# Releasing a pair's attention behind the next block's keys and values in a fused decoder block

## The chip, the core and the metric

The kernel runs on one core of one Trainium2 chip. The metric is the device time of one execution in microseconds (us), lower is better. Engines are named as the profile names them: PE (TensorE, matmuls and transposes; PEld its weight loads), DVE (VectorE), ACT (ScalarE), POOL (GpSimd), SP (SyncE, which issues most DMAs). The program gives each engine its instructions in a fixed order.

## The reference

One decoder layer on 2048 tokens of width 1024, in float32:

```python
h = modulate(rms_norm(x, g_pre_mix), shift_m, scale_m)
proj = h @ w_in          # q_a k_a v_a | q_m k_m v_m o_m | i_m f_m | g_a g_m
q_a, k_a = rope(q_a), rope(k_a)                     # 8 query heads, 2 key heads, 64 wide
y_a = sliding_window_attention(q_a, k_a, v_a, sinks)  # window 128, blocks of 128 tokens
q_m, k_m = silu(causal_conv4(q_m, k_m))
h_m = mlstm_chunkwise(q_m, k_m, v_m, i_m + b_i, f_m + b_f)   # 4 heads, 128 wide
y_m = sigmoid(o_m) * head_layer_norm(h_m)
merged = sigmoid(g_a) * (y_a @ w_branch_attn) + sigmoid(g_m) * (y_m @ w_branch_mlstm)
x = x + gate_m * rms_norm(merged @ w_out)
h2 = modulate(rms_norm(x, g_pre_ffn), shift_f, scale_f)
x = x + gate_f * rms_norm((silu(h2 @ w_ffn_gate) * (h2 @ w_ffn_up)) @ w_ffn_down)
```

A query block of 128 tokens attends to its own keys and those of the block before. The mLSTM's input and forget gates i and f go through a log-sigmoid, a cumulative sum and a running maximum over the tokens before its chunks can start.

## The kernel before

**Precision.** Each float32 operand is split into a high part (a cast on ACT, lines 264, 267 and 1744) and a low part (a subtraction on DVE, lines 265, 268 and 1745); a product is three matmuls (`mm3`), recorded at line 212. Transposes are recorded at line 217.

**Staging.** The tokens are four blocks of 512 (b = 0 to 3), taken in two superblocks sb of a pair b0, b1. `superblock(sb)` is a list of work items in program order: queries of b0 (q0), keys, values and gate pre-activations of b0 (kv0, 264 columns), the mLSTM values of b0 (`vm(b0)`), then kv1, q1 and `vm(b1)` for the other block, then 14 pairs of projection columns (`pairs`, each with a two-by-two fast product over both blocks), then both blocks' outputs. In the first superblock q0 and kv0 were written by hand in `first_block`. A group such as kv1 is `KD * NT` = 32 products of three matmuls, 96 matmuls in all.

**Weights.** In the first two blocks weights come from the inputs, are split and the parts of b1 are stored to HBM (line 374, `w_kv_d`, `w_q_d`, `w_vm_d`); in superblock 1 they are loaded ready split (lines 328 and 333). All these go out on SP's queue in its order. There are two raw buffers (`raw`) and four buffers for split parts (`whi`, `wlo`).

**Attention.** When a token tile of q or k/v leaves its accumulator, a stream rotates it on DVE (`rope`, lines 790 to 793), transposes it on PE and stores it into a per-block tile in HBM, `at_d[n]` (lines 806, 833, 851 and 853). `attend(b)` first forces all these streams to their end (`finish(R["qk"])`), then makes the four 128-token attention blocks of b ready; for b0 it also spawns two `attention_stream`s, one for the even and one for the odd blocks, so that attention runs in pairs of 128-token blocks. A block loads its tile (`at`, line 954, 896 KB, two buffers; line 949 and 952 for the very first), computes 24 score matmuls (`mix<-at`), copies and masks them (lines 985 and 987), takes maxima (993), exponentials on ACT (1002), sums (1003, 1004), a scaling on POOL (1005), transposes, masks (1014, 1018), does the value matmuls (`mix<-tm,at`) and stores `y_d` (1032, 1037). If the block two places on is already released, its tile is loaded at once, from ACT's queue; otherwise the stream waits and loads it from SP's.

**Gates.** `attend(b)` also spawns `gates(b)`: small DVE and ACT operations on `gt`, four transposes, the scans (lines 905 and 909 to 912), transposes of 68 rows and a few exponentials. It reads `gt`, which the next block's k/v evictions overwrite, so it has to come before them.

**What sets the order.** The program is written with a planner's clock: every matmul adds a planned time to `now`, and a spawned stream resumes once `now` has passed its due time (`tick`, the constants `L_...`), so its instructions are woven between the main matmuls. `finish` moves the clock forward until the given streams have ended. The tile framework then orders each engine's instructions by readiness on a modelled timeline, where of several that are ready the one earlier in the program goes first (`schedule_with_timeline_sim=True`); only the first block is held to program order. It also sets all waits.

**Where the results are needed.** `finish(convs + R["gs", b0] + R["gs", b1])` after the eighth projection pair, before the mLSTM starts; `end_attention(NT)` in the fourteenth pair, before `y_d` of b0 is loaded (line 1248); `end_attention(2 * NT)` later still.

**Buffers.** Attention, gates and the second conditioning stream (`ada_stream`, lines 467 and 476) share nine `tm` tiles; four PSUM banks serve as accumulators (`acc`) and four for everything else (`mix`).

Of the kernel before, what the change touches and what calls it, by code (L numbers as in the profile page):

```python
# [73 lines left out]
def decoder_block(ctx: ExitStack, tc: tile.TileContext, a: dict, out: bass.AP, dbg=None):  # L74
# [49 lines left out]
    def tx(shape, dtype=F32):  # L124
        return tpool.tile(shape, dtype, tag="tx", name=nm("tx"), bufs=9)
# [93 lines left out]
    def spawn(gen, delay=0.0):  # L219
        st = [now[0] + delay, gen, False]  # L220
        streams.append(st)
        return st
# [15 lines left out]
    def finish(sts):  # L238
        for st in sts:
            while not st[2]:  # L240
                now[0] = max(now[0], min(q[0] for q in streams))
                tick()
# [190 lines left out]
    b1 = const.tile([P, 48], F32, name="b1")  # L433
# [130 lines left out]
    def hsums(names):  # L564

        for name in names:
            raw = HR.pop(name)
            lo = hc_part(name, 1)
            nc.sync.dma_start(lo.bitcast(F32), raw)
        yield L_HD  # L570
        for name in names:
            hi, lo = (hc_part(name, i) for i in range(2))
            for k in range(4):
                v = lo[:, k, :].bitcast(F32)
                A.copy(hi[:, k, :], v)
                V.tensor_tensor(lo[:, k, :], v, hi[:, k, :].bitcast(F32), op=ALU.subtract)
                yield L_HS
# [191 lines left out]
    def superblock(sb):  # L769
        b0, b1 = 2 * sb, 2 * sb + 1  # L770
# [8 lines left out]
        def rope(raw, heads, b, t):  # L779
            sin, cos = tables[sb]  # L780
            t += (b % 2) * NT
            W = heads * HD
            raw = raw[:, :W]
            src = raw.rearrange("p (h u f) -> p h u f", u=2, f=32)
            cb = cos[:, t, :].unsqueeze(1).to_broadcast([P, heads * 2, 32])
            sb_ = sin[:, t, :].unsqueeze(1).unsqueeze(1).to_broadcast([P, heads, 2, 32])
            z = tx([P, 512])
            zz = z[:, :W].rearrange("p (h u f) -> p h u f", u=2, f=32)
            rr = raw.rearrange("p (h f) -> p h f", f=32)
            V.tensor_tensor(zz, src[:, :, ::-1, :], sb_, op=ALU.mult)  # L790
            V.tensor_tensor(rr, rr, cb, op=ALU.mult)
            V.tensor_tensor(src[:, :, 0, :], src[:, :, 0, :], zz[:, :, 0, :], op=ALU.subtract)
            V.tensor_tensor(src[:, :, 1, :], src[:, :, 1, :], zz[:, :, 1, :], op=ALU.add)
            return raw, z

        def q_stream(b, t, yz):
            yield L_ROPE
            y, z = yz
            pt = mix_tile()
            for j in range(GQ):  # L800
                transpose(pt[:, j * P:(j + 1) * P], y[:, j * P:(j + 1) * P])
            hi, lo = z.bitcast(F32R), y.bitcast(F32R)
            A.activation(hi, pt, AF.Copy, scale=HD ** -0.5)
            V.scalar_tensor_tensor(lo, pt, HD ** -0.5, hi.bitcast(F32), op0=ALU.mult, op1=ALU.subtract)
            for i, q in enumerate((hi, lo)):
                nc.sync.dma_start(at_d[b * NT + t][:, i * 512:(i + 1) * 512], q.bitcast(F32))
# [50 lines left out]
        def q_kv(b):  # L857
            if b > 1:
                q = token_group(kept_weights("q"), KD, 512, lhs_h(b), evac_q(b), kept=True)
            else:  # L860
                q = token_group(srcs_rows(w_in, KD, C_Q), KD, 512, lhs_h(b), evac_q(b), pair_heads=True, store="q" if b else None)
            if b > 1:
                return q, token_group(kept_weights("kv"), KD, 264, lhs_h(b), evac_kv(b), kept=True)
            raw_kv = Raw(load_kv)
            return q, token_group([(raw_kv, (lambda r, j=j: r[:, j:j + 2, :]), j, 2) for j in range(0, KD, 2)], KD, 264, lhs_h(b), evac_kv(b), store="kv" if b else None)

        def vm(b):
            def evac(t, ps):
                v = tx([P, 512])
                A.copy(v, ps)  # L870
                nc.sync.dma_start(vm_d[b][:, t, :], v)
            if b > 1:
                yield from token_group(kept_weights("vm"), KD, 512, lhs_h(b), evac, kept=True)
            else:
                yield from token_group(srcs_rows(w_in, KD, C_VM), KD, 512, lhs_h(b), evac, store="vm" if b else None)
# [69 lines left out]
        def load_at(n, queue):  # L945
            a_ = at()
            af = a_.bitcast(F32)
            if n == 0:
                queue.dma_start(af[:, :AT_K], at_d[n][:, :AT_K])
                for c0, k in ((AT_K, 2), (AT_V, 1)):  # L950
                    v_, d_ = (z[:, c0:c0 + 2 * k * P].rearrange("p (i u k) -> p i u k", i=k, u=2)[:, :, 1, :] for z in (af, at_d[n]))
                    queue.dma_start(v_, d_)
            else:
                queue.dma_start(af, at_d[n])
            return a_
# [86 lines left out]
        def attention_stream(u):  # L1042
            a_ = None
            for i in range(u, 2 * NT, 2):
                n = b0 * NT + i
                if a_ is None:
                    while i >= ready[0]:
                        yield 1000.0
                    a_ = load_at(n, nc.sync)
                    yield L_LOAD  # L1050
                    a_ = yield from attention(n, a_, lambda: i + 2 < ready[0])
                else:
                    yield L_LOAD - 1500.0
                    a_ = yield from attention(n, a_, lambda: i + 2 < ready[0])
                done_att[0] += 1
                yield 500.0
# [3 lines left out]
        def attend(b):  # L1060
            finish(R["qk"])
            ready[0] = (b - b0 + 1) * NT
            if b == b0:
                R["att"] = [spawn(attention_stream(0), L_QK), spawn(attention_stream(1), L_QK + L_ATT2)]
            R["gs", b] = [spawn(gates(b), L_QK)]

        def end_attention(n):
# [285 lines left out]
        if sb == 0:  # L1353
            raws, rotated = {}, {}

            def late_q(t):
                yield from q_stream(b0, t, rope(raws[t], HQ, b0, t))

            def q_raw(t, ps):
                raws[t] = tx([P, 512])  # L1360
                A.copy(raws[t], ps)
                if t > 1:
                    R["qk"].append(spawn(late_q(t), L_KV0 + L_LATE * (t - 1)))

            def q_rope(t):
                rotated[t] = rope(raws[t], HQ, b0, t)

            def q_rest(t):
                for _ in q_stream(b0, t, rotated[t]):
                    pass  # L1370

            first.update(kv=kv0, evac=q_raw, rope=q_rope, rest=q_rest)
        else:
            yield start
            yield from q0
            yield from kv0
            yield lambda: attend(b0)
        yield from vm(b0)
        yield lambda: finish([hps[b1]])
        if sb == 0:  # L1380
            yield lambda: attend(b0)
        yield lambda: hps.update(t=spawn(hsums(("T2", "T4"))))
        q1, kv1 = (list(z) for z in q_kv(b1))
        yield from kv1
        yield from q1
        vm1 = list(vm(b1))
        yield from vm1[:len(vm1) // 4]
        yield lambda: attend(b1)
        yield from vm1[len(vm1) // 4:]

        def start_f():
# [809 lines left out]
    def program():  # L2201
        items = [it for sb in range(NSB) for it in superblock(sb)]
        last = max(i for i, it in enumerate(items) if isinstance(it, Part))
        first_block()
        yield from items[:last]
        yield lambda: next(phase2)
        yield from items[last:]
# [47 lines left out]
```

## Time and profile before

| | us |
|---|---|
| median of 3 runs | 2666.65 |
| lowest, highest | 2666.62, 2668.6 |
| profiled execution, its own time | 2664.19 |
| profiled execution, span from first to last instruction | 2662.2 |
| PE busy in the span | 2614.5 (98%) |
| DVE busy in the span | 1935.3 (73%) |
| ACT busy in the span | 1281.4 (48%) |
| mean granted PE clock | 0.996 |

Times in the profile run from the first instruction of the span. A matmul row counts its modelled duration, and matmuls overlap, so the time from one to the next is read from runs of many in the chain of waits. "x24" counts instructions; `acc<-whi,big` reads "into an accumulator from a weight part and an activation part". A wait row names the engine, what it was to write and its line, then what it waited for.

By their rows the stages of interest lie so in the span: superblock 0 has `vm(b0)` from 74, kv1 from 97 to 119, q1 from 122; superblock 1 has kv0 to 735, `vm(b0)` to 763, kv1 from 766 to 784, q1 from 791 to 838.

### The profile page before, as it was taken

The page shows a single profiled execution, that of the slowest core. Times are in us where ns is not written, and L with a number is a line of the kernel's source. Part 1 is how long each engine was busy: PE and PEld are TensorE (multiplying, and loading weights), DVE is VectorE, ACT ScalarE, POOL GpSimd, SP SyncE. Part 2 cuts the span into 40 slices and gives each one's busy share as a digit, 9 for nine tenths or more (in the row PEclk, how much of TensorE's full clock was granted, in tenths as well). Part 3 has the DMA queues.
Part 4 walks back from the last instruction along what each step waited for, and adds up shares of the span by engine and source line. Part 5 has one row for each costly group of instructions (what it writes and reads, how often), then busy time and mean ns, then how long its engine had stood idle before and what let it go on. Part 6 is the DMA issues. An engine that isn't in the chain of part 4 may idle for free.

```text
span 2662.2 us, 36035 instructions
## 1 busy us (share of the span) xinstructions
PE 2614.5 (98%) x12546; PEld 2142.4 (80%) x12546; DVE 1935.3 (73%) x3758; ACT 1281.4 (48%) x2531; POOL 133.1 (5%) x181
## 2 busy tenths in 40 slices
PE   8999999999989999999999999999999999999998
PEld 6777788888877788888878888888778888888786
DVE  6878887768675988875877777776776767676466
ACT  6656544545654654454643433345544333333444
POOL 0000001101100000110000000000000000000000
PEclk9999999999999999999999999999999999999999
DMA  7794466897797545597766554547675323234556
GB/s 270 255 327 141 135 194 186 266 327 247 263 311 241 179 135 185 181 301 261 224 235 199 172 174 155 165 136 232 211 241 173 111 99 113 94 111 138 191 204 221
DMA packets 352166, 532.95 MB, mean 200 GB/s; under 512 B 23136, under 2 KB 209628, under 8 KB 345200
## 3 DMA queue, kind: packets, MB, share of 16 engines
q1 hardware_dynamic: 333768, 514.86, 57.8%
q10 hardware_dynamic: 18216, 15.79, 1.9%
q8 instruction: 99, 1.62, 0.2%
q14 instruction: 83, 0.68, 0.1%
HBM read 367.61 MB, written 154.57 MB: 196 GB/s over the span
## 4 chain that ended last, share of the span: by engine, by line
PE 88%; DVE 5%; DMA 4%; ACT 2%; issue 1%; POOL 0%; ACTq 0%; SPq 0%; DVEq 0%; POOLq 0%
PE acc L212 61%; PE mix L212 23%; PE mix L217 2%; DVE hl L1745 1%; PE acc L90 1%; PE mix L90 1%; ACT hl L1744 1%; DMA raw<-as_d 1%; ACT tm L1002 1%; DMA raw<-ws_d 0%; DMA raw<-w_kv_d 0%; DMA big<-in_x_dram 0%; DMA raw<-in_w_ffn_down_dram 0%; DMA at_d<-tx 0%; DMA raw<-in_w_in_dram 0%
## 5 line engine op out<-in xcount | busy, mean ns | idle before, releaser
L212 PE MATMUL acc<-big,hl 128*128 128x512 f32 x3936 | 936.0, 392 | 4.0 <-ACT hl L1744 1.8
L212 PEld LDWEIGHTS acc<-big,hl 128*128 128x128 f32 x3936 | 732.3, 188 | 164.4 <-issue 5.1
L1744 ACT CAST hl<-raw 128x512 fp32r<-128x512 f32 x732 | 439.9, 621 | 491.7 <-PE acc L212 216.3
L1745 DVE TENSOR_TENSOR hl<-raw,hl 128x512 fp32r<-128x512 f32 x732 | 496.6, 695 | 200.7 <-ACT hl L1744 197.1
L212 PE MATMUL acc<-whi,big 128*128 128x512 f32 (+1 forms) x896 | 279.3, 387 | 0.1
L212 PE MATMUL mix<-big,hl 128*128 128x512 f32 x1056 | 263.0, 390 | 1.8 <-ACT hl L1744 1.1
L212 PE MATMUL acc<-hl,hl 128*128 128x512 f32 x1008 | 237.3, 393 | 5.8 <-DVE hl L1745 3.0
L212 PEld LDWEIGHTS mix<-big,hl 128*128 128x128 f32 x1056 | 197.7, 188 | 44.6 <-ACT hl L1744 2.0
L212 PEld LDWEIGHTS acc<-hl,hl 128*128 128x128 f32 x1008 | 187.0, 188 | 51.5 <-DVE hl L1745 8.7
L212 PEld LDWEIGHTS acc<-whi,big 128*128 128x128 f32 x896 | 167.2, 189 | 33.3 <-ACT whi L264 0.4
L212 PE MATMUL mix<-hl,hl 128*128 128x512 f32 x792 | 182.6, 391 | 2.6 <-ACT hl L1744 1.8
L212 PEld LDWEIGHTS mix<-hl,hl 128*128 128x128 f32 x792 | 147.9, 188 | 36.5 <-ACT hl L1744 3.0
L212 PE MATMUL acc<-wlo,big 128*128 128x512 f32 (+1 forms) x448 | 173.4, 388 | 1.1 <-DVE wlo L265 1.1
L212 PE MATMUL acc<-big,whi 128*128 128x512 f32 x512 | 157.4, 393 | 0.0
L268 DVE TENSOR_TENSOR wlo<-raw,whi 128x1024 fp32r<-128x1024 f32 (+1 forms) x76 | 91.2, 1200 | 60.9 <-ACT whi L267 55.7
L267 ACT CAST whi<-raw 128x1024 fp32r<-128x1024 f32 (+1 forms) x76 | 78.3, 1031 | 93.9 <-PE acc L212 87.3
L492 POOL TENSOR_TENSOR rs<-ms,halves 128x1 f32<-128x1 f32 (+1 forms) x56 | 41.0, 739 | 1635.8 <-DVE ms L490 1589.2
L212 PE MATMUL mix<-hcT4h,hl 128*128 128x512 f32 x352 | 115.6, 389 | 0.7 <-ACT hl L1744 0.7
L212 PE MATMUL acc<-hcT2h,hl 128*128 128x512 f32 x352 | 115.5, 389 | 0.0
L212 PEld LDWEIGHTS acc<-big,whi 128*128 128x128 f32 x512 | 95.3, 188 | 19.3
L212 PEld LDWEIGHTS acc<-wlo,big 128*128 128x128 f32 x448 | 85.0, 190 | 18.8 <-DVE wlo L265 1.4
L212 PE MATMUL acc<-big,wlo 128*128 128x512 f32 x256 | 97.5, 392 | 0.0
(379 smaller groups left out, 3640.7 us busy)
## 6 DMA issues: line engine op xcount, KB each, us to landing
as_d<-w SPq DMA_DIRECT2D x154, 256.0 KB, 2.0
raw<-in_w_in_dram SPq DMA_DIRECT2D x36, 1024.0 KB, 5.4
raw<-as_d SPq DMA_DIRECT2D x70, 512.0 KB, 3.8
raw<-in_w_ffn_gate_dram SPq DMA_DIRECT2D x22, 1024.0 KB, 5.6
raw<-in_w_ffn_up_dram SPq DMA_DIRECT2D x22, 1024.0 KB, 6.0
raw<-ws_d SPq DMA_DIRECT2D x40, 512.0 KB, 4.7
tx<-in_w_ada_dram SPq DMA_DIRECT2D x64, 256.0 KB, 5.3
g_d<-tx SPq DMA_DIRECT2D x64, 256.0 KB, 4.5
```

The lines of the kernel that those rows point to most:

```text
L90: self.last = tc.keep_in_program_order(f(*p, **k)).ins
L212: T.matmul(o, lhsT=lhsT, rhs=rhs, start=start, stop=stop, skip_group_check=resumed)
L217: T.transpose(o, i, ident[:k, :k])
L267: A.copy(hv, src)
L268: V.tensor_tensor(lv, src, hv.bitcast(F32), op=ALU.subtract)
L492: G.tensor_tensor(r[:, :n], ms[:, :n], nhalf[:, :n], op=ALU.pow)
L1002: A.activation(sc[jj][:, i, :], sc[jj][:, i, :], AF.Exp, bias=nm_[:, c:c + 1], accum_out=sums[:, c:c + 1])
L1744: A.copy(v(hi), src)
L1745: V.tensor_tensor(v(lo), src, v(hi).bitcast(F32), op=ALU.subtract)
```

## The change

`attend(b)` is cut in two: `attend` keeps the forced finishing, the release and the two streams; the new `gate(b)` holds the spawning of `gates(b)`. Where `attend(b0)` stood, `gate(b0)` stands now: behind kv0 in superblock 1, behind `vm(b0)` in superblock 0. `attend(b0)` itself stands behind kv1 in both, ahead of q1. For b1 both are called where `attend(b1)` was, after the first quarter of `vm(b1)`.

```diff
             if b == b0:
                 R["att"] = [spawn(attention_stream(0), L_QK), spawn(attention_stream(1), L_QK + L_ATT2)]
+
+        def gate(b):
             R["gs", b] = [spawn(gates(b), L_QK)]
...
             yield from q0
             yield from kv0
-            yield lambda: attend(b0)
+            yield lambda: gate(b0)
         yield from vm(b0)
         yield lambda: finish([hps[b1]])
         if sb == 0:
-            yield lambda: attend(b0)
+            yield lambda: gate(b0)
         yield lambda: hps.update(t=spawn(hsums(("T2", "T4"))))
         q1, kv1 = (list(z) for z in q_kv(b1))
         yield from kv1
+        yield lambda: attend(b0)
         yield from q1
         vm1 = list(vm(b1))
         yield from vm1[:len(vm1) // 4]
-        yield lambda: attend(b1)
+        yield lambda: (attend(b1), gate(b1))
         yield from vm1[len(vm1) // 4:]
```

So the release of b0's attention moves past kv1 in superblock 0, and past `vm(b0)` and kv1 in superblock 1. The forced finishing at that place now also takes in the key streams of b1, which kv1 has just spawned. No instruction is added or removed.

## The prediction

> **What bounds the kernel now.** I read the page first, for what the end hangs on. Its first and fourth parts:
>
> ```profile
> PE 2614.5 (98%) x12546; PEld 2142.4 (80%) x12546; DVE 1935.3 (73%) x3758; ACT 1281.4 (48%) x2531; POOL 133.1 (5%) x181
> PE 88%; DVE 5%; DMA 4%; ACT 2%; issue 1%; POOL 0%; ACTq 0%; SPq 0%; DVEq 0%; POOLq 0%
> ```
>
> TensorE (PE) is the bound: 88% of the chain of waits is PE's own work. The change adds and removes no instruction of it, so it can win or lose only where PE stands still or runs at half clock. The second view is therefore the table of stretches around the moved work. Columns: length, then PE, PE weight loads, DVE, ACT and POOL busy, granted PE clock, DMA share, GB/s.
>
> ```profile
> 103.30:119.10 15.80, 14.17 (x104) 12.86 (x102) 13.10 (x40) 5.95 (x17) 0.00 (x0) 0.78 0.99 342
> 106.80:113.50 6.70, 5.77 (x32) 5.44 (x33) 6.58 (x19) 1.75 (x4) 0.00 (x0) 0.50 0.97 329
> 119.10:123.90 4.80, 1.35 (x8) 0.65 (x6) 2.91 (x12) 4.80 (x23) 2.19 (x2) 0.99 0.31 110
> 123.80:127.10 3.30, 3.24 (x10) 2.75 (x11) 2.19 (x10) 3.30 (x18) 1.56 (x2) 0.50 0.71 289
> 762.00:784.30 22.30, 19.25 (x131) 18.00 (x130) 16.29 (x51) 12.61 (x41) 2.35 (x2) 0.85 0.96 371
> 765.50:772.30 6.80, 6.13 (x35) 6.03 (x35) 4.79 (x10) 2.18 (x4) 0.00 (x0) 0.50 1.00 420
> 784.30:791.20 6.90, 3.91 (x30) 2.17 (x30) 6.44 (x31) 5.95 (x27) 1.14 (x2) 1.00 1.06 356
> 791.20:840.00 48.80, 48.80 (x276) 36.22 (x275) 23.48 (x62) 19.77 (x62) 5.63 (x6) 1.00 0.61 193
> 855.00:900.00 45.00, 42.99 (x230) 32.98 (x230) 44.19 (x98) 32.25 (x85) 4.28 (x4) 1.00 0.65 219
> ```
>
> PE idles 3.45 us in 119.1 to 123.9 (4.80 less 1.35), 2.99 us in 784.3 to 791.2, and three times its clock is 0.50. All this lies where the first pair of attention blocks of a superblock meets the other block's keys and values (kv1 below: 96 matmuls of 264 columns). Whom PE waited for, in the stretches 100 to 130, 755 to 792, 131 to 755 and 792 to 960, one fence each (total us, times, longest):
>
> ```profile
> PE mix L217 <- POOL tm L1005: 2.2, 1, 2.2
> PE mix L217 <- DVE tm L912: 1.6, 1, 1.6
> PE acc L212 <- DVE wlo L265: 1.1, 1, 1.1
> ```
>
> ```profile
> PE acc L212 <- DMA raw<-w_kv_d: 3.0, 1, 3.0
> PE mix L217 <- POOL tm L1005: 1.9, 1, 1.9
> PE mix L212 <- DVE tm L1018: 0.9, 2, 0.5
> PE mix L212 <- DMA at<-at_d: 0.9, 1, 0.9
> ```
>
> ```profile
> PE mix L217 <- POOL tm L1005: 1.7, 2, 1.3
> ```
>
> ```profile
> PE mix L217 <- POOL tm L1005: 0.3, 1, 0.3
> ```
>
> The softmax tail (L1005) holds PE 2.2 and 1.9 us at the two first pairs of a superblock, but 1.7 + 0.3 us at the six other pairs together with nothing else of attention: 0.33 us a pair. So a pair is cheap when it does not run beside kv1.
>
> What half clock costs is read from the chain of waits, where a piece is a run of matmuls of one kind:
>
> ```profile
> 108.42 2.86 PE mix L212 x18
> 111.28 4.13 PE acc L212 x24
> 123.86 1.65 PE acc L212 x3
> 126.57 2.65 PE acc L212 x10
> 143.22 3.50 PE mix L212 x33
> 286.39 67.79 PE acc L212 x298
> 766.17 4.30 PE acc L212 x18
> 770.92 2.26 PE mix L212 x18
> 778.48 6.06 PE acc L212 x48
> ```
>
> At full clock a matmul of 264 columns takes 0.126 us (6.06/48), one of 512 columns 0.227 (67.79/298), a score matmul 0.106 (3.50/33). So the half clock after 106.8 cost 4.13 - 24 x 0.126 = 1.1 and 2.86 - 18 x 0.106 = 0.95, that after 123.8 cost 1.65 - 3 x 0.227 = 0.97 and 2.65 - 10 x 0.227 = 0.4, together 3.4 us; that after 765.5 cost 2.0 + 0.35 = 2.4 us.
>
> **The change part by part.** *First superblock: scores move from inside kv1 to behind it.* kv1 is cut up by 48 score matmuls (24 a block). They bring DVE work, and the last weight split of kv1 stands behind it; the load of q1's first weights stands on SP behind the store of that split. DVE's groups in 108 to 114, and SP in time:
>
> ```profile
> L993 DVE TENSOR_REDUCE mx<-tm 128x4 f32<-128x512 f32 x3 | 2.0, 667 | 0.0
> L987 DVE COPY_PREDICATED_SCALAR tm<-m_prev,negc 128x256 f32 x4 | 1.7, 482 | 0.0
> L987 DVE COPY_PREDICATED tm<-m_prev,mix 128x256 f32<-128x256 uint32 x3 | 1.3, 425 | 0.0
> ```
>
> ```profile
> 114.57 0.32 SPq L374 DMA_DIRECT2D w_kv_d<-wlo  x1
> 114.94 0.43 SPq L298 DMA_DIRECT2D raw<-in_w_in_dram  x1
> ```
>
> Without those 5.0 us on DVE the split, the store and q1's weights come up to 5.0 us sooner, and the scores fill PE between kv1 and q1 instead of delaying both. Term 1, the idle 3.45: ends -3.45 and 0; I take -2.5, since DVE holds other work that moves up. Term 2, the half clocks, 3.4: ends -3.4 and 0; half, -1.7, as one of the two follows the wait for L1005 and L265, and the other the gates' wait. Term 3, that gates' wait (L912, 1.6): the gates keep their place, so 0; end -1.6.
>
> *Second superblock: past the values and kv1.* The two loads of attention tiles stand on SP just ahead of kv1's weights:
>
> ```profile
> 753.27 1.15 SPq L954 DMA_DIRECT2D at<-at_d  x2
> 754.48 0.43 SPq L333 DMA_DIRECT2D raw<-w_kv_d  x1
> ```
>
> ```profile
> at<-at_d SPq DMA_DIRECT2D x7, 896.0 KB, 8.1
> ```
>
> At the 371 GB/s of the table 896 KB last 2.5 us, so two loads hold the weights up by 4.9 us, more than the 3.0 us that PE waits for them. Term 4, the waits for these weights (3.0) and for the attention tile itself (0.9): at best both go, -3.9. If the weights land when they do now, the 0.9 becomes waiting for weights and the 24 scores that PE does ahead of them (2.5 us at 0.106) no longer fill that time: +2.5. I take -2.4, nearer to the first, since the loads then belong to later work. Term 5, the half clock after it, 2.4: ends -2.4 and 0; half, -1.2. Term 6, the idle 2.99 at 784.3, where kv1's evictions and rotations meet the softmax on DVE (6.44 of 6.90 busy): ends -2.99 and 0; -2.5, leaving what a pair costs elsewhere.
>
> *What the new place costs (term 7).* Two pairs run in q1, the second quarter of the values and the first projection pairs. At least 0.33 us each: +0.7; at most what their tails cost now, 3.45 + 2.99: +6.4. In 791 to 840 DVE has half its time free (23.48 of 48.80 busy), so I take +2.0, nearer the lower end.
>
> *At nothing.* The forced finishing now takes kv1's key streams behind kv1: four transposes, eight small ACT and DVE operations and eight stores. q1's matmuls, ready by then, hide them; without that cover PE waits for the four key rotations, which are less than the 6.44 us of DVE work in 784.3 to 791.2 that holds them: say +4. In the second superblock block b0's q and k streams are no longer forced ahead of the values; the 96 matmuls there cover them as now. The gates' DVE chain loses its competitor. The attention loads of the next pair may go out on ACT's queue instead of SP's, if the second release comes before the pair ends; what ACT then holds up is covered by PE's four accumulators. The end of attention is late next, but nobody waits for it: its last store against the first load of its results:
>
> ```profile
> L1032 ACTq DMA_DIRECT2D y_d<-tm x16: 366/378/1019, 134.0 to 954.2; - x16
> L1248 SPq DMA_DIRECT2D big<-y_d x16: 319/400/688, 488.7 to 1243.8; - x16
> ```
>
> *The sum.* -2.5 - 1.7 - 2.4 - 1.2 - 2.5 + 2.0 = -8.3 us. Against the profiled execution of 2664.19 us that is 2655.9; the median of the runs, 2666.65, lies 2.46 above that execution, so 2658.4 for the median. All good ends together give -17.0 (-3.45 - 3.4 - 1.6 - 3.9 - 2.4 - 2.99 + 0.7), 2650; all bad ends +12.9, 2679.5.
>
> A rule speaks against term 2: the Trainium skill, "TensorE: Matmul & The Clock Gate", section "Why this matters for your kernels", lets the clock fall to half after about 3 us of idle PE. The trace differs: half clock follows waits of 1.6 us and of 2.2 + 1.1 us too. By the rule only the 3.0 us wait would count, term 2 would not be had, and the sum would be -6.6.
>
> Another speaks against term 4: the Trainium skill, "DMA: Bandwidth & Descriptors", section "Issuing engines are not separate DMA queues", says that transfers of all queues share the same 16 engines. The trace agrees (DMA share 0.96 to 1.06 in 762 to 791). By it the 4.9 us of tile loads would press on q1's weights instead, term 4 would be 0 and the sum -5.9.
>
> **The rivals.** *Nothing really moves.* The framework orders each engine by readiness, not by place in the program: block 0's tile is loaded at 76.4 us, 20 us ahead of its place behind the values.
>
> ```profile
> 76.43 0.32 SPq L949 DMA_DIRECT2D at<-at_d  x1
> ```
>
> If the loads go out where they do now and the scores slip into kv1 again, the time is the old one, 2666. Against it: of two ready matmuls the earlier in the program goes first, and that is now kv1's.
>
> *The gain is given back on DVE.* In the second superblock the release moves by the values and kv1 (96 x 0.227 + 96 x 0.126 = 34 us). If the second pair thus falls behind 855, where DVE has 0.81 us of 45 free, its 5.0 us of score work comes 4.2 us late, and PE waits for the same engine's splits: 2658.4 + 4.2 = 2662.6.
>
> *Slower: the scores were the filler.* The weights of kv1 and q1 may come when they do now, because raw buffers and SP's order decide it. Then PE reaches those waits with less done: the second superblock loses 2.5 us and its idle grows to 6 us, with one more half clock (+2.4); the first idles for the 48 scores that it did meanwhile (48 x 0.106 = 5.1), with one more half clock (+1.4). 2.5 + 2.4 + 5.1 + 1.4 - 2.5 (term 6 is had all the same) = +8.9: 2675.5. It decides if the weights come less than 2.5 us sooner; for it speaks that the loads of both stand behind stores and full buffers, against it the 5.0 and 4.9 us just named.
>
> **How the numbers follow.** No change and a change of 0.2% (5.3 us) can't be told apart here. The forecast has 0.52 (0.47 of it faster by more than that, 0.05 within), the old order 0.15 and the given-back gain 0.12 (0.01 faster), the filler 0.21. So faster 0.48, same 0.31, slower 0.21. The forecast's own range is 2650 to 2663; the range to hold 8 in 10 goes on to 2674, which takes in half of the slower case.
>
> **What would show it.** Terms 1 and 2: the stretch from the last kv1 matmul to q1 without idle, q1's first load on SP clearly before 114.9, the clock above 0.78. Term 4: the attention tiles' loads on SP behind kv1's weights, no PE wait for them. Term 6: no wait of over 1 us for L1005 or L1018. Term 7: PE busy in q1. It is wrong if PE waits for weights longer than now, if a half clock appears in a new place, or if PE idles in 855 to 900 beyond today's 2.0 us.

## The result, and the profile after

The changed kernel takes 2685.04 us (median of 5 runs, 2683.73 to 2687.35). Its time over that of the kernel before is 1.0069, 95% interval 1.0057 to 1.0080: about 18 us slower than the 2666.65 from which the forecast was made, where 8.3 us faster was forecast. Five runs of the kernel before, 2666.65 among them, have their median at 2668.60 (2666.62 to 2670.24). The time lies above the upper end of the range, 2674, and above the sum of all bad ends, 2679.5.

The busy times on the page after have the same number of instructions on every engine as before, and PE is still the bound:

```profile
PE 2629.9 (98%) x12546; PEld 2150.0 (80%) x12546; DVE 1939.6 (72%) x3758; ACT 1282.0 (48%) x2531; POOL 135.3 (5%) x181
```

The profiled execution after took 2687.35 us, its span 2685.4. To place the loss, both spans are cut at the same five events: the first matmul of `vm(b0)` in the first superblock, the first matmul of the projections (`acc<-big,hl`), the first matmul of the second superblock, its first projection matmul, and the first matmul of the feed-forward part. So the first and third stretch hold keys, values, queries and most of the attention; the second and fourth hold the projections, the mLSTM and the rest of the attention. Columns as in the prediction's table. Before, then after:

```profile
73.80:189.28 115.48, 109.59 (x617) 87.62 (x615) 91.02 (x238) 69.31 (x191) 9.01 (x9) 0.96 0.84 292
189.28:697.56 508.28, 506.43 (x2498) 417.26 (x2499) 390.84 (x829) 266.86 (x520) 41.68 (x41) 1.00 0.66 216
697.56:853.58 156.02, 149.12 (x871) 122.73 (x870) 101.50 (x280) 78.52 (x214) 15.93 (x19) 0.98 0.81 277
853.58:1366.66 513.08, 511.07 (x2539) 421.35 (x2538) 407.80 (x829) 277.40 (x543) 42.55 (x40) 1.00 0.64 213
```

```profile
77.44:195.35 117.91, 105.98 (x578) 85.67 (x576) 86.75 (x229) 64.87 (x180) 6.61 (x7) 0.91 0.82 280
195.35:710.22 514.87, 514.87 (x2540) 421.42 (x2539) 397.18 (x837) 271.50 (x531) 44.81 (x44) 1.00 0.65 215
710.22:866.11 155.89, 148.11 (x844) 122.88 (x842) 102.15 (x281) 80.00 (x217) 15.17 (x18) 0.97 0.82 284
866.11:1386.08 519.97, 519.13 (x2569) 424.79 (x2568) 409.54 (x828) 275.97 (x540) 44.73 (x41) 1.00 0.64 208
```

The four stretches changed by +2.4, +6.6, -0.1 and +6.9 us, together 15.8. The two spans differ by 23.2, some 5 more than the medians; the other 7.4 lie ahead of the first mark (3.6) and behind the last (3.8), where no line was changed.

The matmul counts are what the reader should look at. The first stretch does 39 matmuls less than before (578 against 617) and still takes 2.4 us more: PE stood still for 117.91 - 105.98 = 11.9 us instead of 115.48 - 109.59 = 5.9, and its mean clock fell from 0.96 to 0.91. The third does 27 less in the same time. These matmuls are the tail of this work: 20 and 16 of them value matmuls of attention, the others small transposes for attention, for q1's rotated tiles and for the gates. They are then done among the projections, where the second and fourth stretch have 42 and 30 more. Read so, the loss arises ahead of the projections, and is hidden there by work put off; the kernel released half way, below, where nothing is put off, bears this out.

Whom PE waited for after the change, from 100 to 330 and from 755 to 870 (total us, times, longest):

```profile
PE mix L212 <- DMA at<-at_d: 4.1, 1, 4.1
PE mix L217 <- DVE tm L912: 3.2, 1, 3.2
PE mix L217 <- POOL tm L1005: 2.2, 2, 1.9
PE acc L212 <- ACT tx L840: 1.1, 1, 1.1
PE acc L212 <- DVE wlo L268: 0.7, 1, 0.7
PE mix L217 <- DVE tm L987: 0.4, 1, 0.4
```

```profile
PE mix L217 <- DVE tx L793: 3.0, 3, 1.6
PE mix L212 <- DVE tm L922: 2.6, 1, 2.6
PE acc L212 <- ACT tx L870: 1.7, 1, 1.7
PE acc L212 <- DMA raw<-w_kv_d: 0.4, 1, 0.4
```

The waits that the prediction wanted gone are gone: the softmax tail between kv1 and q1, and all but 0.4 of the 3.0 us for kv1's weights. Others came in their place. The largest lies at the end of `vm(b1)` in the first superblock. PE in order of time there, before and then after:

```profile
183.28 0.39 PE L212 MATMUL acc<-whi,big 128*128 128x512 f32 x1
...
189.28 10.95 PE L212 MATMUL acc<-big,hl 128*128 128x512 f32 x47 [0.81 <-ACT tx L870]
```

```profile
177.64 0.50 PE L212 MATMUL acc<-whi,big 128*128 128x512 f32 x1
182.24 3.61 PE L212 MATMUL mix<-at 64*128 64x256 f32 x24 [4.10 <-DMA at<-at_d]
186.21 1.12 PE L217 MATMUL mix<-ident,tx 128*128 128x128 f32 x4 [0.36 <-DVE tm L987]
189.19 1.12 PE L217 MATMUL mix<-ident,tm 128*128 128x128 f32 x4 [1.87 <-POOL tm L1005]
...
195.35 2.83 PE L212 MATMUL acc<-big,hl 128*128 128x512 f32 x11
```

From the last value matmul to the first projection matmul it is now 17.7 us instead of 6.0. In it PE first waits for a pair's tile, then for its softmax, and runs at half clock for 13.7 us, as the table of that stretch says:

```profile
181.80:195.50 13.70, 10.52 (x53) 7.31 (x54) 9.86 (x28) 9.67 (x40) 2.45 (x3) 0.50 0.18 64
```

### The profile page after: what moved, and what is told of

Read it like the earlier page. It is cut to its first block, busy times and chain, and to the rows that moved or that the text cites. A ratio compares the mean times of both kernels' runs of the same rounds, so it can differ in the third digit from the quotient of the medians.

```text
span 2685.4 us, 36053 instructions
## 1 busy us (share of the span) xinstructions
PE 2629.9 (98%) x12546; PEld 2150.0 (80%) x12546; DVE 1939.6 (72%) x3758; ACT 1282.0 (48%) x2531; POOL 135.3 (5%) x181
## 4 chain that ended last, share of the span: by engine, by line
PE 59%; DVE 4%; DMA 3%; ACT 1%; issue 1%; POOL 0%; SPq 0%; DVEq 0%; POOLq 0%; ACTq 0%
PE acc L212 39%; PE mix L212 19%; DVE hl L1748 1%; PE mix L217 1%; ACT hl L1747 1%; DMA raw<-as_d 1%; DMA raw<-in_w_ffn_down_dram 1%; DMA raw<-ws_d 0%; DMA x<-tm 0%; DVE big L1748 0%; DMA x<-tx 0%; DVE w L2058 0%; DMA raw<-in_w_ffn_gate_dram 0%; DVE big L2071 0%; POOL rs L492 0%
## 5 line engine op out<-in xcount | busy, mean ns | idle before, releaser
L212 PEld LDWEIGHTS acc<-wlo,big 128*128 128x128 f32 x448 | 85.3, 190 | 17.7 <-DVE wlo L268 1.2
```

The source lines that it names most:

```text
L212: T.matmul(o, lhsT=lhsT, rhs=rhs, start=start, stop=stop, skip_group_check=resumed)
```

## The experiments

In all of them the kernel before ran beside (2665.86 to 2666.89 us); a ratio is the kernel's time over that of before.

**Which superblock.** The change in the first superblock alone, and in the second alone:

```diff
             yield from q0
             yield from kv0
-            yield lambda: gate(b0)
+            yield lambda: (attend(b0), gate(b0))
...
         yield from kv1
-        yield lambda: attend(b0)
+        if sb == 0:
+            yield lambda: attend(b0)
```

That is the kernel with the change in the first alone. The other has `(attend(b0), gate(b0))` behind `vm(b0)` of the first superblock, and `if sb == 1` behind kv1.

> Only the first superblock has the change (attention of b0 released behind kv1); the second releases it behind kv0 as before. The two profiles put about 9 us of the loss into the first superblock (the time from the start of its values to the start of the next superblock grew by 9.0) and about 7 into the second. If the two losses are separate: before + 9 us, 2676 to 2680. If the loss comes from the second superblock alone, or only from both together: within 3 us of before. If a change of order anywhere costs by chance, no rule: either half could give any amount.

> Only the second superblock has the change (release behind the values and kv1). If the losses are separate: before + 7 us, 2674 to 2678, with PE waiting about 3 us for the rotation of kv1's keys (L793) right behind kv1 and a half clock there. If the scores were needed as filler for kv1's weights (my rival), PE should wait for weights for 3 us or more ahead of kv1. If all comes from the first superblock: 2668.

Measured: 2672.31 us for the first alone, ratio 1.0018 (1.0010 to 1.0027), and 2675.36 for the second alone, 1.0033 (1.0021 to 1.0046). Both halves lose. The first lost less than the 9 us expected of it; the second came as expected, with waits of 2.2 and 1.2 us for the key rotations and only 0.3 for kv1's weights. Their 5.6 and 8.7 us add to 14.3, a little below the interval of the whole loss (15 to 21 us); with the intervals of the two halves the sum and the whole overlap, and whether something comes only from both together stays open. What spoils the change is found in each superblock, and not only in the values that the second release alone jumps over.

**The forced finishing.** The prediction put at nothing that the forced finishing now takes kv1's key streams too. The changed kernel, with only those streams forced that are older than kv1:

```diff
-        def attend(b):
-            finish(R["qk"])
+        def attend(b, own=None):
+            finish(list(R["qk"]) if own is None else own)
...
+        mine = []
+        yield lambda: mine.extend(R["qk"])
         yield from kv1
-        yield lambda: attend(b0)
+        yield lambda: attend(b0, mine)
```

> The changed kernel, but the forced finishing behind kv1 takes only the streams that existed ahead of kv1, not kv1's own key streams. If forcing these streams is what costs the second superblock (waits of 3.0 us for L793 and the half clock of 6.8 us that follows): 2685 - 5, 2678 to 2682, and no wait for L793. If the time is lost anyway because PE has nothing else ready there (filler): the wait turns up under another name and the time stays 2683 to 2687.

Measured: 2687.25 us, 1.0074 (1.0060 to 1.0087), no better. The wait for the key rotations is still there, from 690 to 1370:

```profile
PE mix L217 <- DVE tx L793: 3.5, 2, 2.5
```

Not forcing the streams does not take them out of the way: the key transposes still stand ahead of the first scores (131.29 to 132.79 against 136.42 in the first superblock), as their due time comes before that of the scores.

**The queue of the tile loads.** The next pair's tile may go out on ACT's queue. The changed kernel with that load on SP's:

```diff
-                later = load_at(n + 2, nc.scalar)
+                later = load_at(n + 2, nc.sync)
```

> The changed kernel, but the attention tile of the block two places on is issued from SP's queue instead of ACT's. In the changed kernel PE waited 4.1 us for such a tile at 182 and then ran at half clock for 13.7 us. If ACT's queue, held up by a wait for a round trip of the sums, is the cause: that wait goes and the time falls by 5 to 10 us, to 2675 to 2680. If the cause is that blocks 2 and 3 fall into a gap where PE has no other work: PE waits there for something else (softmax), and the time stays above 2681.

Measured: 2686.02 us, 1.0075 (1.0062 to 1.0087). In place of the 4.1 us for the tile there is now a wait of the same length for the maxima of the softmax (100 to 205):

```profile
PE mix L212 <- DVE mx L994: 4.2, 1, 4.2
```

So the queue of the tile's load is not the cause; the pair waits at that place for something else.

**Buffers between q1, the values and the projections.** After the change the values' evictions (L870) at the end of the first superblock's `vm(b1)` come late. They take a `tx` tile; q1's rotated tiles, also `tx`, are held until their transposes. ACT's last of these evictions, before and then after the change:

```profile
188.65 1.56 ACT L870 COPY tx<-acc 128x512 f32<-128x512 f32 x3
...
190.55 0.59 ACT L870 COPY tx<-acc 128x512 f32<-128x512 f32 x1 [0.34 <-DMA at_d<-tx]
```

```profile
192.32 0.59 ACT L870 COPY tx<-acc 128x512 f32<-128x512 f32 x1
...
196.47 1.05 ACT L870 COPY tx<-acc 128x512 f32<-128x512 f32 x2
...
198.73 0.59 ACT L870 COPY tx<-acc 128x512 f32<-128x512 f32 x1 [1.20 <-DMA at_d<-tx]
```

The values of all blocks but the first (`if b`) were given a tile of another pool, `ld`, in the changed kernel and in the one before:

```diff
-                v = tx([P, 512])
+                v = ld([1, 512])[:, 0, :] if b else tx([P, 512])
```

> The changed kernel, but the evicted mLSTM values of blocks 1 to 3 go to the four tiles of the group that is idle then (ld) instead of the nine shared ones (tx). New theory: in the first superblock q1's rotated tiles hold eight of the nine tx tiles until attention gives up a PSUM bank for their transposes; the values' evictions (L870) wait for tx, and the first projection pair waits for the accumulators that they free; the later the pair of blocks 2 and 3, the longer. If so the evictions come at 175 to 181 instead of 192 to 199, the projections start about 10 us earlier, and the time falls by 6 to 10 us, to 2675 to 2680. Rival (pile-up: PE has nothing else because the projections' weights are late): 2683 to 2688.

> The kernel before with the same other tiles for the values. By the theory of the chain of tiles there is little to win, as the evictions there came at 188.7 right behind the pair of blocks 2 and 3 and PE waited 1.0 us for them: 2663 to 2667. By the rival: 2665 to 2669.

Measured: changed kernel 2674.82 us, 1.0029 (1.0020 to 1.0038); kernel before 2663.16, 0.9984 (0.9975 to 0.9992). In the changed kernel the projections then start 3.4 us after the last value matmul (176.35), with the wait on the evictions at 2.85:

```profile
179.71 4.64 PE L212 MATMUL acc<-big,hl 128*128 128x512 f32 x10 [2.85 <-ACT ld L870]
```

The shared pool is thus a part of the loss: the edit takes 10.2 us off the changed kernel, but 3.5 to 3.7 off the one before, so by difference some 6.5 of the 18 us come from what the change adds to the pressure on that pool. The order is not mended by it: the scores still come at 134.30, behind the key transposes (129.18 to 130.67). The kernel before with this edit is also the best of all that were run, 0.16% below the kernel before.

**Attention ahead of kv1's keys.** The kernel with only its own streams forced, and kv1's key streams (block b1) due after 10,000 of the planner's units instead of 2,100, so that the scores precede them in the program (their stream starts 1,500 after the release and allows 5,000 for its tile's load); and the same with the values apart:

```diff
-            yield L_ROPEK
+            yield L_ROPEK if n // NT % 2 == 0 else 10000.0
```

> The changed kernel, where only the streams older than kv1 are forced and the key streams of b1 fall due 10000 planned ns after their eviction instead of 2100, so that their transposes stand behind a good part of q1 and not ahead of it. If PE lost its 4.5 us (waits for L793) and most of the half clock there because the transposes stand ahead of q1: 2685 - 6, 2677 to 2682. If the loss of the second superblock is the missing filler in kv1 (waits for L870 and L922 inside kv1): 2682 to 2687.

> Both: the values' evictions in other tiles, and the key transposes later. If the two are the whole loss: 2668 to 2674. If something else is lost in either superblock: above 2676.

Measured: 2668.44 us, 1.0003 (0.9994 to 1.0012), and 2668.04, 1.0003 (0.9994 to 1.0012). One number taken up, against the run with own streams alone, brings 18.8 us back, far more than the 6 expected, though attention is still released behind kv1. With late keys the values' edit adds nothing (0.4 us), so the two gains are not separate parts of the loss. The stretches of the kernel with late keys:

```profile
74.63:187.41 112.78, 105.01 (x577) 85.15 (x575) 85.95 (x225) 62.22 (x166) 6.80 (x6) 0.95 0.84 289
187.41:700.44 513.03, 513.03 (x2540) 421.78 (x2539) 399.02 (x843) 274.42 (x544) 45.53 (x44) 1.00 0.65 216
700.44:854.60 154.16, 146.74 (x843) 121.90 (x842) 104.79 (x285) 81.16 (x220) 15.15 (x18) 0.98 0.85 290
854.60:1369.38 514.78, 514.78 (x2567) 424.37 (x2566) 405.86 (x824) 274.88 (x537) 43.56 (x41) 1.00 0.64 209
```

Its matmul counts are those of the changed kernel within 2, in all four stretches, but they take 5.1, 1.8, 1.7 and 5.2 us less. So it is not the number of matmuls put off into the projections that costs, but what PE did while they were put off and where they then fall.

**The place of the release.** If the place of the scores against kv1's key transposes decides, then a release earlier in kv1 has to help, and the forced finishing alone must not matter much. The release after half of kv1, after a quarter of it, and the kernel before with only the forced finishing added behind kv1:

```diff
-        yield from kv1
+        yield from kv1[:len(kv1) // 2]       # // 4 in the other kernel
         yield lambda: attend(b0)
+        yield from kv1[len(kv1) // 2:]
```

```diff
         yield from kv1
+        yield lambda: finish(R["qk"])        # in the kernel before
         yield from q1
```

> The changed kernel, but the attention of b0 is released in the middle of kv1 (after 48 of its 96 matmuls) instead of behind it. Theory A (what counts is where the first pair's scores come against kv1: inside it they give PE work while its weights, evictions and gates are late): the scores of the first pair come some 10 us earlier than in the changed kernel and part of the loss returns, 2670 to 2679 us. Rival B (what counts is the forced finishing or the move past the values, not the place in kv1): still 2682 to 2688. Rival C (any place ahead of the last key transposes is as good as the old one): 2664 to 2669.

> As the run before, but released after the first quarter of kv1 (24 of 96 matmuls). Theory A: the time falls further with the place, 2666 to 2673 us, below the run with half of kv1 ahead. Rival B: still 2682 to 2688. Rival C: 2664 to 2669, like the run before.

> The kernel before with only the forced finishing of the query and key streams added behind kv1, nothing of attention moved. Theory A: the scores keep their place, so the time of before, 2664 to 2670 us. The prediction's bound for the forced finishing without cover: +4, 2671.

Measured: half 2681.70 us, 1.0058 (1.0046 to 1.0071); quarter 2665.58, 0.9998 (0.9989 to 1.0007); the forced finishing alone 2671.00, 1.0016 (1.0008 to 1.0025). The half was expected at 2670 to 2679, the forced finishing alone at no more than 2670; both came slower. The place does not act by degrees. Between a quarter and a half of kv1 nearly the whole loss comes at once, and the profiles show what changes there. The first superblock's first scores, and the first or last of kv1's key transposes beside them, in the kernel before, in those released at a quarter, with late keys, at half, and in the changed kernel:

```profile
103.42 1.44 PE L212 MATMUL mix<-at 64*128 64x128 f32 x21
...
125.31 0.41 PE L217 MATMUL mix<-ident,tx 128*128 128x128 f32 x1
```

```profile
110.59 2.82 PE L212 MATMUL mix<-at 64*128 64x128 f32 x18
...
126.02 0.27 PE L217 MATMUL mix<-ident,tx 128*128 128x128 f32 x1
```

```profile
109.90 2.82 PE L212 MATMUL mix<-at 64*128 64x128 f32 x18
...
125.77 0.27 PE L217 MATMUL mix<-ident,tx 128*128 128x128 f32 x1
```

```profile
127.65 0.27 PE L217 MATMUL mix<-ident,tx 128*128 128x128 f32 x1
127.85 1.55 PE L212 MATMUL mix<-at 64*128 64x128 f32 x18
```

```profile
131.95 0.27 PE L217 MATMUL mix<-ident,tx 128*128 128x128 f32 x1
...
135.59 1.57 PE L212 MATMUL mix<-at 64*128 64x128 f32 x24
```

In the two kernels as fast as before, the scores run 15 us ahead of the first key transpose, inside kv1, as they do in the kernel before (22 us ahead). In the two slow ones they stand behind a key transpose: behind the first of the four with a half (the other three follow from 132.76 on), behind the last in the changed kernel. In the second superblock it is the same: first scores at 772.85 and first key transpose at 785.14 with a quarter, 772.18 against 784.16 with late keys, 791.95 against 790.18 with a half, 796.21 against 793.70 in the changed kernel. The loads of the first pair's tile do not explain it: in the first superblock of the changed kernel the last of them goes out at 100.54, 35 us ahead of the scores.

The stretches of the kernel released at a quarter, whose time is that of before:

```profile
75.27:194.53 119.26, 110.27 (x617) 88.43 (x615) 90.50 (x238) 69.48 (x191) 9.80 (x9) 0.96 0.83 281
194.53:700.97 506.44, 506.05 (x2498) 417.29 (x2499) 393.37 (x829) 266.70 (x520) 42.14 (x41) 1.00 0.65 217
700.97:854.27 153.30, 146.51 (x871) 122.19 (x870) 108.43 (x287) 82.34 (x221) 16.59 (x19) 0.99 0.85 292
854.27:1365.13 510.86, 509.93 (x2538) 421.86 (x2539) 405.83 (x822) 274.13 (x536) 43.24 (x40) 1.00 0.64 211
```

It has the counts of the kernel before: nothing is put off into the projections. In this one execution its second superblock is 4.9 us shorter up to the feed-forward part (2.7 and 2.2), its first 1.9 longer.

The kernel released half way has these counts too, within three, and so nothing hides its loss:

```profile
74.26:201.25 126.99, 113.86 (x618) 88.74 (x616) 91.43 (x236) 68.52 (x189) 9.57 (x9) 0.92 0.79 265
201.25:708.69 507.44, 507.44 (x2501) 417.53 (x2499) 393.85 (x831) 267.40 (x522) 42.71 (x41) 1.00 0.65 217
708.69:866.71 158.02, 148.61 (x872) 122.01 (x870) 106.92 (x289) 82.65 (x221) 15.66 (x19) 0.98 0.83 284
866.71:1381.18 514.47, 512.70 (x2538) 422.89 (x2539) 404.45 (x820) 273.84 (x535) 42.68 (x40) 0.99 0.64 209
```

Its first stretch alone is 11.5 us longer than before. Up to the last value matmul it takes as long as the kernel released at a quarter (105.3 us to 179.53, 104.9 us to 180.16), with 548 matmuls done against 556. From there to the projections it takes 21.7 us against 14.4, and 6.0 before the change. So, by these two executions, the loss of the first superblock lies for the most part not in kv1, from which the scores are missing, but at the end of the values, where the second pair comes late.

The forced finishing alone cost 5.1 us by the medians (2 to 7 by the interval), and its wait for kv1's weights is about as before (3.4 us); where else it loses stays open, beside one wait of 2.4 us for a split (L1746) among the second superblock's projections.

**Both helpful edits on the kernel before.** Values apart and late keys, with the release in its old place:

> The kernel before with the two edits that helped the changed kernel: the values of the second block leave their accumulators through another pool, and the key streams of the second block wait for their planned time until far behind kv1. Theory A: in the kernel before the scores are inside kv1 already, so late keys add nothing to the 2663.2 us of the values' edit alone: 2661 to 2665. Rival: late keys free PE behind kv1 (the waits for L1005 and the key rotations, some 3 us in each superblock): 2657 to 2660.

Measured: 2665.16 us, 0.9995 (0.9986 to 1.0004), 2 us above the values' edit alone. Late keys helped only where attention is released behind kv1.

## Why the prediction was wrong

*Term 1, the idle between kv1 and q1 of the first superblock (-2.5):* right. Of 3.45 us there is left the 1.1 for L840.

*Term 4, waits for kv1's weights and for the tile (-2.4):* right, and a little more: 3.0 fell to 0.4, and the 0.9 for the tile to nothing in that stretch. On SP the first load of kv1's weights now stands ahead of both tiles (764.80 against 768.66 and 770.66), the second between them (769.53); that this order is the cause was not tried by itself. The rule of the Trainium skill that was set against it ("DMA: Bandwidth & Descriptors", section "Issuing engines are not separate DMA queues": the transfers of all queues share 16 engines) was read there as putting the term at 0; the fall from 3.0 to 0.4 doesn't bear out that reading. The sharing itself is not contradicted (DMA share 1.03 in 772.8 to 791.8).

*Term 6, L1005 and L1018 at 784 (-2.5):* right in its waits. In 755 to 870 no wait for either is left in the list. But the waits for L793, L922 and L870 came in place of terms 4 and 6: all that PE waited in 750 to 870 fell only from 8.5 to 7.7 us.

*Term 3, the gates' wait L912 (0):* wrong, +1.6 (from 1.6 to 3.2). The gates kept their place and DVE lost its competitor; that PE, with no scores in between, came to it sooner is the likely reason. The gates' next step shows it too, L922 with 2.6 us in the second superblock, in a list that had no such row before.

*Terms 2 and 5, the half clocks (-1.7 and -1.2):* wrong. They moved and grew; the first stretch fell to 0.91 from 0.96. The largest, 13.7 us, lies where the prediction named no risk, though it named a half clock in a new place as a sign of being wrong. Of the rule cited there (the Trainium skill, "TensorE: Matmul & The Clock Gate", section "Why this matters for your kernels": half clock after about 3 us of idle PE) this execution bears out so much, that the long half clock follows the wait of 4.1 us.

*The step that failed is term 7 together with "at nothing".* Term 7 took +2.0 us for the pairs' new place, between +0.7 and +6.4, and took it for granted that the scores come right behind kv1 and there fill PE. They came behind kv1's key transposes instead, which wait for DVE (3.0 us in three waits in the second superblock), and in the first superblock 14 us into q1 (135.59 against 121.56). That moves a whole pair of attention on, by 28.5 us in the first superblock (103.42 to 135.59, less the 3.6 of the later start), and the pair behind it meets the end of `vm(b1)`. There PE has nothing else: the tile and softmax waits (4.1 and 2.2), nearly all of the 13.7 us at half clock and the first of the evictions kept up by `tx` tiles lie in those 17.7 us. "The end of attention is late next, but nobody waits for it" was right of waits and wrong of time: the 42 and 30 matmuls left over were done among the projections, at +6.6 and +6.9 us in those stretches. How much of this is the matmuls' own time was not measured by a run; that the same number of them costs 1.8 and 5.2 us less with late keys shows that it isn't all their own time.

*The cover of the forced finishing.* The prediction allowed +4 if q1's matmuls should not hide the key streams. The kernel before pays 5 us for the forced finishing alone, about that price, where the prediction took nothing. In the changed kernel it is no term of its own, since taking it away gave nothing; the key streams' place ahead of the scores was, with up to 18.8 us.

*The rival "the scores were the filler" (2675.5)* had the sign and perhaps a part of the mechanism: with the scores gone from kv1, PE waited for the gates, the evictions and the key rotations. But it hung on the weights' coming late, and they came in time. Its price of +8.9 left out the second pair, the end of the values and the work put off. *"Nothing really moves"* fell: the scores didn't slip back into kv1 (they do so with late keys, at 109.90 and 772.18, and there the old time returns). Its reason against was right in kind, though what counted as earlier in program order, as far as the runs show, were kv1's key transposes rather than its matmuls. *"Given back on DVE"* fell too; the one wait for splits there after the change is 0.6 us.

The runs show that the scores' place ahead of or behind the key transposes goes with the loss: ahead in both superblocks the kernels take 2663.2 to 2671.0 us, behind in one 2672.3 and 2675.4, behind in both 2674.8 to 2687.3. They show that the due time of those transposes alone (own streams against late keys) removes it, and that the `tx` tiles carry about 6.5 us of it. But first scores ahead of the transposes always lie inside or ahead of kv1, and first scores behind them always behind it, so the runs don't part "late" from "missing in kv1"; for the first superblock the stretches of the kernels released at a quarter and half way speak for "late", for the second it stays open. That a pair so held back makes the first stretch longer is read from the profiles. That the scores are held behind the transposes by the PSUM tiles that both take in program order is only argued; more of these tiles weren't tried.

## What to carry to other kernels

Before a block of work is moved, look at what will then stand directly ahead of it in program order, and for what that waits: here a pair of attention came to stand behind four small transposes that wait for DVE, and the due time of those transposes gave the whole loss back. Waits removed are not yet time gained: nearly all that the forecast named went, and the work that used to cover the next waits went with them. When a stage ends early, count its instructions: 39 matmuls less in 2.4 us more was the loss, though the later stretch shows the larger number.

## What the runs showed that was not expected

A release after 24 of 96 matmuls cost nothing (0.9998), one after 48 cost 0.58% and one after all 96 0.69%: a step, not a slope. Half clock lasted 13.7 us without a break in 181.8 to 195.5, through 52 narrow matmuls and transposes with PE busy 10.5 us of it, and ended only as the projections' wide matmuls began; once it had begun no wait was over 1.87 us (L1005), but for the rest of the 4.1. And another pool for one kind of tile was worth more than any move of the order that was tried: 0.16% on the kernel before.
